# Laying the operand tiles of a split-float32 trunk at one residue modulo 512 bytes

## The chip, the cores and the metric

The kernel runs on one core of one Trainium2 chip. The metric is the device time of one execution in microseconds (us), lower is better; it is the median of several runs. A profile is one separate execution, recorded instruction by instruction.

## The reference, cut to what matters

One sequence of 512 tokens with 1024 channels goes through two layers, all in float32:

```python
# layer 0: RWKV-7 time mixing (six projections 1024x1024 or low rank, a recurrence per head of 64)
x = layer_norm(ALPHA * x + time_mix(x)) ; x = layer_norm(ALPHA * x + mlp(x, w1[0], w2[0]))
# layer 1: differential attention over shared K/V with a T5 bias, 16 score maps, 8 heads of 128
q = x @ w_q ; k, v = split(x @ w_kv)
attn = softmax(q1 k1 + bias) - lam * softmax(q2 k2 + bias)     # block-causal
x = layer_norm(ALPHA * x + (subln(attn @ v)) @ w_o) ; x = layer_norm(ALPHA * x + mlp(x, w1[1], w2[1]))
# mlp(x, w1, w2) = square(relu(x @ w1)) @ w2, w1 1024x4096, w2 4096x1024
```

## The kernel before

**Three products for one.** Every dense product is made of three TensorE matmuls on operands that were split into a high and a low part of type float32r (`split`, lines 105 to 107): high times high (line 141), high times low (line 142), low times high (line 143), all inside `mm3`. The first argument of a matmul is stationary (it is loaded into the array, 128 columns of 4 bytes, so 512 bytes in each partition), the second one is moving (512 or 256 columns). Three such matmuls are called a triple here.

**Where weights go.** `unit` loads 128x1024 weights into a `wst` tile (pool `ws`, 3 buffers), ScalarE rounds them into `whi` (line 106), and VectorE or GpSimd writes the rest into `wlo` (line 107). `whi` and `wlo` come from pool `wp` (4 buffers each) and, inside an MLP, four units in turn from pool `w4` (4 buffers each) and four from `wp`, beginning with `w4`. In the first MLP product and the attention projections the weights are stationary and `ba` (the transposed input, high and low) moves; in the second MLP product the activations `hh` and `hl` are stationary and the weights move; in attention's output product `yh` and `yl` are stationary and the weights move. Attention's scores use `qT` (stationary) and `kT` (moving).

**The first product after a norm** is computed in two halves of 256 tokens (`proj_halves`), so that it can begin before the last two token blocks are normalised: 288 matmuls of 256 columns in an MLP, 192 in attention.

**Where tiles lie.** SBUF pools are stacks: a pool opened later lies behind those still open, on memory of pools that are closed. A pool lays its tags one behind the other in the order of first use, each with its number of buffers, sizes rounded up to 32 bytes. `t` (line 83) asks for 128-byte alignment for the tags in `ALIGNED`; such a tag takes a further 128 bytes of its pool, so that `wlo`, `hl` and `yl` begin 128 bytes off where `whi`, `hh` and `yh` do. In the program as built, the tiles begin at these residues modulo 512: `ba` 384; `whi`/`wlo` in `w4` 256/384, in `wp` 384/0; `hh`/`hl` 0/128; `yh`/`yl` 256/384; `kT` and `qT` 128; in the first layer's projections the inputs `bb` 128, `bc` 160, `acc` 0 and the weights 256. Slices inside a tile are multiples of 512 bytes.

**What lies on what.** Attention's one pool `att` covers bytes 70656 to 174976: small set-up tiles (`rb`, `br`, `lm`, ...), `kT`, `qT`, `vt`, `bt`, and so on, with `yh` and `yl` last (150272 to 174976). The second MLP's pool `h` and its `w4` (140544 to 173440) lie on the same bytes, as the first MLP's do before attention. The order of the instructions on each engine is set by a scheduler that simulates the program; a tile in reused memory also waits for the last readers of what lay there.

**Order around the change.** The program is: first layer (`rwkv`), MLP 0 (`mlp(0, 1)`), attention, MLP 1. Attention projects groups of two heads (`P0` to `P3`), computes pairs (`p0` to `p3`), adds the output product of heads 0 to 3 in between (`o01`, `o23`), and ends with that of heads 4 to 7, one token block after the other, with the layer norm of each block behind it.

Of the kernel before, what the change touches and what calls it, by code (L numbers as in the profile page):

```python
# [9 lines left out]
F32R = mybir.dt.float32r  # L10
# [8 lines left out]
P = 128  # L19
D = 1024  # L20
T = 512
NT = T // P
# [3 lines left out]
HD = 64  # L26
NPAIR = 8
WCOL = 256
LINE = 128
ALIGNED = ("ba", "acc", "bb", "whi", "wlo", "hh", "hl", "yh", "yl")  # L30
ALPHA = 4.0 ** 0.25
CDEC = math.exp(-0.5)
GN_EPS = 64e-5
# [33 lines left out]
class Trunk:  # L67
# [15 lines left out]
    def t(self, pool, tag, shape, dt=F32, bufs=None):  # L83
        self.n += 1
        kw = {} if bufs is None else {"bufs": bufs}
        if tag in ALIGNED:
            kw["align_bytes"] = LINE
        return pool.tile(list(shape), dt, tag=tag, name=f"{tag}_{self.n}", **kw)

    def mul(self, eng, out, in0, in1):  # L90
# [59 lines left out]
    def setup(self):  # L150
        nc, a = self.nc, self.a
        cp = self.pool("const")
        self.cp = cp
        self.cst = self.t(cp, "cst", [P, NCST])
        self.cv = self.t(cp, "cv", [P, NVEC, NK])
        nc.sync.dma_start(out=self.cv, in_=a["cvec"])
        self.ident = self.cst[:, C_ID:C_ID + P]
        self.dr = self.pool("dr", space=DRAM)

    def wunit(self, src, kh, lo_eng=None):  # L160
# [10 lines left out]
    def rwkv(self):  # L171
# [12 lines left out]
        with ExitStack() as ph:  # L184
# [4 lines left out]
            ip = self.pool("inv", 1, ctx=ph)  # L189
# [178 lines left out]
            acc, wst, wos = [], {}, {}  # L368
# [52 lines left out]
            for step in PLAN.split():  # L421
# [21 lines left out]
                with ExitStack() as pri:  # L443
                    if off is not None:
# [3 lines left out]
                     "f": lambda g, b: self.finish(cm2, ep, psE, g, grp[g], b),  # L448
                     "l": load, "c": conv, "w": wo, "n": norm}[op](*z)
        self.lnp = self.pool("ln", 1, side="right")  # L450
        self.ws = self.pool("ws", 3, side="right")
        self.wp = self.pool("wp", 4, side="right")
        self.psT, self.tT = self.pool("psT", 2, space=PSUM), "t"
# [46 lines left out]
    def inverse(self, ip, GU, nbD, gbD, E):  # L500
        nc = self.nc
        V, S, G, PE = nc.vector, nc.scalar, nc.gpsimd, nc.tensor
        NU = self.t(ip, "nu", [P, 32, 32], bufs=2)
        nb = nbD.rearrange("u b s t -> (u b) (s t)")
        nc.sync.dma_start(out=NU.rearrange("p s t -> p (s t)"),
                          in_=bass.AP(tensor=nb.tensor, offset=nb.offset, ap=[[0, 2], [1024, 64], [1, 1024]]))
        for s in range(31):
            n, m = 31 - s, s // 2 + 1
            tm = self.t(ip, "gtm", [P, 144], bufs=3)
            tmv = tm[:, 0:m * n].rearrange("p (i t) -> p i t", t=n)  # L510
            gv = GU[:, 0:m, s + 1:32]
            E.tensor_tensor(out=tmv, in0=GU[:, 0:m, s:s + 1].to_broadcast([P, m, n]),  # L512
                            in1=NU[:, s:s + 1, s + 1:32].to_broadcast([P, m, n]), op=ALU.mult)
            E.tensor_tensor(out=gv, in0=gv, in1=tmv, op=ALU.add)  # L514
        for r in range(2):
            nc.sync.dma_start(out=gbD.rearrange("u b (j r) t -> r (u b) j t", r=2)[r], in_=GU[64 * r:64 * r + 64])
# [329 lines left out]
    def attention(self):  # L846
        nc, a = self.nc, self.a
        V, S, G, PE = nc.vector, nc.scalar, nc.gpsimd, nc.tensor
        with ExitStack() as ph:
            ap = self.pool("att", 1, ctx=ph)  # L850

            def ps_a():
                return self.t(self.psA, "a", [P, T])
# [31 lines left out]
            def project(g):  # L885
                wk = self.weight(a["kv"][g], G)
                wq = self.weight(a["q"][g], G)
                pss = self.proj_halves([wk, wq]) if g == 0 else None
                for i in range(4):
                    if g:  # L890
                        ps = ps_a()
                        self.proj_T((wk, wq)[i // 2], i % 2 * P, ps)
                    else:
                        ps = pss[i]
                    h = 2 * g + i % 2
                    if i < 2:
                        kt[h] = []
                        for s in range(2):
                            k = self.t(ap, "kT", [P, 2, T], F32R, bufs=7)
                            S.copy(out=k[R[s], 0], in_=ps[R[s]])  # L900
                            V.tensor_tensor(out=k[R[s], 1], in0=ps[R[s]], in1=k[R[s], 0], op=ALU.subtract)
                            nc.sync.dma_start(out=k[R[1 - s]].bitcast(F32), in_=k[R[s]].bitcast(F32))
                            kt[h].append(k)
                    else:
                        q = self.t(ap, "qT", [P, 2, T], F32R, bufs=4)
                        for s in range(2):
                            S.activation(out=q[R[s], s], in_=ps[R[s]], func=AF.Copy, scale=-SCALE)
                            V.scalar_tensor_tensor(out=q[R[1 - s], s], in0=ps[R[s]], scalar=-SCALE, in1=q[R[s], s],  # L908
                                                   op0=ALU.mult, op1=ALU.subtract)
                        qt[h] = q  # L910
                w = self.weight(a["kv"][4 + g], G)
                vt = self.t(ap, "vt", [P, NT, WCOL], bufs=2)
                for tt in range(NT):
                    ps = ps_a()
                    for k in range(NK):
                        self.mm3(ps[:, 0:WCOL], tuple(z[:, tt * P:(tt + 1) * P] for z in self.xk(k)), w[k],
                                 k == 0, k == NK - 1)
                    S.copy(out=vt[:, tt, :], in_=ps[:, 0:WCOL])
                vts[g] = vt
# [42 lines left out]
            def pair(g):  # L962
                bts = [bias(2 * g + f) for f in range(2)]
                pos = [self.t(self.psX, "o", [P, NT, P]) for _ in range(2)]
                ss = self.t(ap, "ss", [P, 2, NT], bufs=2)
                z = self.t(ap, "z", [P, 2, 2, NT], bufs=2)
                orow = [self.t(ap, "or", [P, NT, P], bufs=2) for _ in range(2)]
                for i in range(0, NT, NTAIL):
                    qbs = QB[i:i + NTAIL]
                    for qb in qbs:  # L970
                        for f in range(2):
                            block(2 * g + f, bts[f], pos[f], z, qb)
                        for f in range(2):
                            jk = self.t(ap, "jk", [P, P], bufs=2)
                            S.activation(out=jk, in_=pos[f][:, qb, :], func=AF.Square, accum_out=ss[:, f, qb:qb + 1])
                    sl = slice(min(qbs), max(qbs) + 1)
                    v = self.t(ap, "zi", [P, 2, NT], bufs=2)[:, :, sl]
                    V.scalar_tensor_tensor(out=v, in0=z[:, 0, :, sl], scalar=SUBLN_EPS, in1=z[:, 0, :, sl], op0=ALU.mult, op1=ALU.mult)
                    V.scalar_tensor_tensor(out=v, in0=ss[:, :, sl], scalar=1.0 / P, in1=v, op0=ALU.mult, op1=ALU.add)
                    rs = self.rsqrt(ap, "ar", v, [P, 2, len(qbs)])  # L980
                    for f in range(2):
                        for qb in sorted(qbs):
                            S.activation(out=orow[f][:, qb, :], in_=pos[f][:, qb, :], func=AF.Copy, scale=rs[:, f, qb - sl.start:qb - sl.start + 1])
                for f in range(2):
                    pt = self.t(self.psT, "t", [P, NT, P])
                    for qb in range(NT):
                        PE.transpose(pt[:, qb, :], orow[f][:, qb, :], self.ident)
                    hi = self.t(ap, "yh", [P, NT, P], F32R, bufs=6)
                    lo = self.t(ap, "yl", [P, NT, P], F32R, bufs=6)
                    S.activation(out=hi, in_=pt, func=AF.Copy, scale=sg)  # L990
                    V.scalar_tensor_tensor(out=lo, in0=pt, scalar=sg, in1=hi, op0=ALU.mult, op1=ALU.subtract)
                    ys[2 * g + f] = (hi, lo)
# [19 lines left out]
            for step in ATT.split():  # L1012
                hs = tuple(map(int, step[1:]))
                if step[0] == "o":
                    out_all(hs, 1.0 if done else ALPHA)
                    done.update(hs)
                else:
                    {"P": project, "p": pair}[step[0]](*hs)
# [92 lines left out]
```

## Time and profile before

| | us |
|---|---|
| median of 3 runs | 1554.7 (1552.41 to 1555.03) |
| profiled execution, its own time | 1556.39 |
| its span, first to last instruction | 1554.6 |
| TensorE matmul busy | 1418.8 (91%) |
| VectorE / ScalarE / GpSimd busy | 836.6 / 559.8 / 430.2 |

Matmuls are pipelined, so the length shown for one overlaps the next; a rate is read from one start to the next. The granted clock (PEclk) is a share of 2.4 GHz; half of it is 1.2 GHz.

### The profile page before, as it was taken

How to read it: one execution, taken by the hardware profiler on the slowest of the kernel's cores; microseconds unless marked ns; L12 is line 12 of the kernel's file. 1: busy time of each engine (PE TensorE's matmuls, PEld its weight loads, DVE VectorE, ACT ScalarE, POOL GpSimd, SP SyncE). 2: the span in 40 equal slices, each digit the busy share in tenths (PEclk: the TensorE clock that was granted, in tenths of full speed). 3: DMA queues.
4: the chain of work that ended last, by engine and by line, in shares of the span. 5: the costliest groups of instructions: out<-in, count | busy, mean ns of one | idle time of the engine just before them, and what ended most of it. 6: DMA issues, size and time to landing. Idle time of an engine off the chain costs nothing.

```text
span 1554.6 us, 21838 instructions
## 1 busy us (share of the span) xinstructions
PE 1418.8 (91%) x8296; PEld 1149.0 (74%) x8296; DVE 836.6 (54%) x1668; ACT 559.8 (36%) x1074; POOL 430.2 (28%) x383
## 2 busy tenths in 40 slices
PE   7879898966899699999999989999987999999997
PEld 2547587755766598888888887888876988888886
DVE  8965475665967853333333543456667433333346
ACT  2333343242333452322324244566445414232220
POOL 5764233273334430100101153322215201010010
PEclk9989889766889899999999999999988999999999
DMA  5245462324221343232323044323102433333311
GB/s 164 75 123 153 114 149 86 103 74 129 64 80 42 108 150 101 89 102 88 102 88 104 6 129 129 84 66 109 62 28 85 161 96 93 97 94 96 94 41 54
DMA packets 89121, 148.15 MB, mean 95 GB/s; under 512 B 34313, under 2 KB 48041, under 8 KB 89017
## 3 DMA queue, kind: packets, MB, share of 16 engines
q1 hardware_dynamic: 89016, 146.76, 31.9%
q8 instruction: 65, 1.06, 0.3%
q14 instruction: 40, 0.32, 0.1%
HBM read 127.74 MB, written 10.57 MB: 89 GB/s over the span
## 4 chain that ended last, share of the span: by engine, by line
PE 71%; DVE 15%; DMA 7%; ACT 2%; POOL 2%; issue 2%; SPq 1%; DVEq 0%; POOLq 0%; ACTq 0%
PE a L141 10%; PE a L142 10%; PE a L143 10%; PE o L142 5%; PE o L143 5%; PE o L141 5%; PE s L142 5%; PE s L143 5%; PE s L141 5%; DMA nu<-nbD 3%; PE e L474 1%; DVE ba L265 1%; PE o L960 1%; DVE gtm L512 1%; DVE gu L514 1%
## 5 line engine op out<-in xcount | busy, mean ns | idle before, releaser
L106 ACT CAST whi<-wst 128x1024 fp32r<-128x1024 f32 (+1 forms) x208 | 195.0, 949 | 356.9 <-PE a L143 139.5
L107 DVE TENSOR_TENSOR wlo<-wst,whi 128x1024 fp32r<-128x1024 f32 x120 | 151.1, 1259 | 231.5 <-ACT whi L106 231.5
L107 POOL TENSOR_TENSOR wlo<-wst,whi 128x512 fp32r<-128x512 f32 (+1 forms) x88 | 166.7, 1909 | 245.0 <-ACT whi L106 236.8
L91 POOL TENSOR_TENSOR r<-r 128x512 f32<-128x512 f32 x64 | 69.0, 1079 | 534.9 <-ACT hh L820 532.4
L822 DVE TENSOR_TENSOR hl<-r,hh 128x512 fp32r<-128x512 f32 x64 | 45.8, 717 | 147.3 <-POOL r L91 147.3
L141 PE MATMUL a<-ba,whi 128*128 128x512 f32 (+1 forms) x336 | 122.5, 366 | 2.2 <-DVE qT L908 2.2
L143 PE MATMUL a<-ba,wlo 128*128 128x512 f32 (+1 forms) x336 | 123.7, 369 | 0.0
L142 PE MATMUL a<-ba,whi 128*128 128x512 f32 (+1 forms) x336 | 123.2, 367 | 0.0
L143 PE MATMUL s<-ba,wlo 128*128 128x512 f32 (+1 forms) x232 | 82.2, 355 | 0.0
L142 PE MATMUL s<-ba,whi 128*128 128x512 f32 (+1 forms) x232 | 81.9, 353 | 0.2 <-DVE ba L107 0.2
L141 PE MATMUL a<-whi,ba 128*128 128x256 f32 x256 | 76.4, 298 | 5.8 <-ACT ev L315 3.2
L141 PE MATMUL s<-ba,whi 128*128 128x512 f32 (+1 forms) x232 | 80.9, 350 | 0.0
L142 PE MATMUL a<-wlo,ba 128*128 128x256 f32 x256 | 75.5, 295 | 0.0
L141 PEld LDWEIGHTS a<-ba,whi 128*128 128x128 f32 x336 | 64.7, 193 | 13.7 <-issue 2.2
L143 PE MATMUL a<-whi,ba 128*128 128x256 f32 x256 | 74.7, 292 | 0.0
L141 PE MATMUL o<-ba,whi 128*128 128x512 f32 (+1 forms) x200 | 71.8, 359 | 2.2 <-ACT ba L106 2.2
L143 PE MATMUL o<-ba,wlo 128*128 128x512 f32 (+1 forms) x200 | 72.6, 363 | 0.0
L142 PE MATMUL o<-ba,whi 128*128 128x512 f32 (+1 forms) x200 | 72.5, 363 | 0.0
L142 PEld LDWEIGHTS a<-ba,whi 128*128 128x128 f32 x336 | 64.2, 191 | 10.3
L143 PEld LDWEIGHTS a<-ba,wlo 128*128 128x128 f32 x336 | 64.2, 191 | 9.9
L141 PE MATMUL o<-whi,hh 128*128 128x512 f32 x176 | 69.3, 394 | 0.0
L142 PE MATMUL o<-wlo,hh 128*128 128x512 f32 x176 | 69.1, 393 | 0.0
(376 smaller groups left out, 3545.9 us busy)
## 6 DMA issues: line engine op xcount, KB each, us to landing
wst<-in_m SPq DMA_DIRECT2D x128, 512.0 KB, 3.9
wst<-in_kv SPq DMA_DIRECT2D x16, 512.0 KB, 4.3
wst<-in_wk SPq DMA_DIRECT2D x16, 256.0 KB, 3.4
wst<-in_wr SPq DMA_DIRECT2D x16, 256.0 KB, 3.5
wst<-in_wv SPq DMA_DIRECT2D x16, 256.0 KB, 4.0
wst<-in_q SPq DMA_DIRECT2D x8, 512.0 KB, 4.7
kT<-kT SPq DMA_DIRECT2D x16, 256.0 KB, 4.6
wst<-in_wo SPq DMA_DIRECT2D x8, 512.0 KB, 3.3
```

The lines of the kernel that those rows point to most:

```text
L91: return eng.tensor_tensor(out=out, in0=in0, in1=in1, op=ALU.mult)
L106: self.nc.scalar.copy(out=hi, in_=src)
L107: (lo_eng or self.nc.vector).tensor_tensor(out=lo, in0=src, in1=hi, op=ALU.subtract)
L141: mm(ps, lh, rh, start=first, stop=False)
L142: mm(ps, lh, rl, start=False, stop=False)
L143: mm(ps, ll, rh, start=False, stop=last)
L265: V.scalar_tensor_tensor(out=mx, in0=xx, scalar=cv[:, V_MU + i, c:c + 1], in1=x0, op0=ALU.mult, op1=ALU.add)
L474: PE.matmul(ps[:, c, :], d["bk"][hs, 4 * b + c].rearrange("p a t -> p (a t)"), d["ar"][hs, 4 * b + c].rearrange("p a t -> p (a t)"), start ...
L512: E.tensor_tensor(out=tmv, in0=GU[:, 0:m, s:s + 1].to_broadcast([P, m, n]), in1=NU[:, s:s + 1, s + 1:32].to_broadcast([P, m, n]), op=ALU.mult)
L514: E.tensor_tensor(out=gv, in0=gv, in1=tmv, op=ALU.add)
L822: V.tensor_tensor(out=hl, in0=r, in1=hh, op=ALU.subtract)
L960: PE.matmul(po[:, qb, :], at[:, kb, :], vt[:, kb, f * P:(f + 1) * P], start=(kb == 0), stop=(kb == qb))
```

## The change

Alignment by request goes away. Instead, three pads shift whole pools: 46 floats at the end of the pool `const`, 8 floats at the start of the pool `ln`, and a scratch tile of the first layer that is 32 bytes smaller (three buffers). Attention's matmul operands `kT`, `qT`, `yh` and `yl` move to a pool of their own, `attq`, opened before `att`. No instruction of any engine is added or removed apart from this.

```diff
-LINE = 128
-ALIGNED = ("ba", "acc", "bb", "whi", "wlo", "hh", "hl", "yh", "yl")
@@ t
-        if tag in ALIGNED:
-            kw["align_bytes"] = LINE
@@ setup
         self.ident = self.cst[:, C_ID:C_ID + P]
+        self.t(cp, "pad", [P, 46])
@@ rwkv
         self.lnp = self.pool("ln", 1, side="right")
+        self.t(self.lnp, "pad", [P, 8])
@@ inverse
-            tm = self.t(ip, "gtm", [P, 144], bufs=3)
+            tm = self.t(ip, "gtm", [P, 136], bufs=3)
@@ attention
+            aq = self.pool("attq", 1, ctx=ph)
             ap = self.pool("att", 1, ctx=ph)
...
-                            k = self.t(ap, "kT", [P, 2, T], F32R, bufs=7)
+                            k = self.t(aq, "kT", [P, 2, T], F32R, bufs=7)
...
-                        q = self.t(ap, "qT", [P, 2, T], F32R, bufs=4)
+                        q = self.t(aq, "qT", [P, 2, T], F32R, bufs=4)
...
-                    hi = self.t(ap, "yh", [P, NT, P], F32R, bufs=6)
-                    lo = self.t(ap, "yl", [P, NT, P], F32R, bufs=6)
+                    hi = self.t(aq, "yh", [P, NT, P], F32R, bufs=6)
+                    lo = self.t(aq, "yl", [P, NT, P], F32R, bufs=6)
```

## Rows read from the trace of the kernel before

**Rows 1.** the page's parts 1 and 4: busy time, and the chain that ended last
```profile
PE 1418.8 (91%) x8296; PEld 1149.0 (74%) x8296; DVE 836.6 (54%) x1668; ACT 559.8 (36%) x1074; POOL 430.2 (28%) x383
...
PE 71%; DVE 15%; DMA 7%; ACT 2%; POOL 2%; issue 2%; SPq 1%; DVEq 0%; POOLq 0%; ACTq 0%
```
**Rows 2.** windows by stage: us, busy and count per engine, PEclk, DMA share, GB/s
```profile
0.00:550.00 550.00, 455.20 (x3492) 341.73 (x3492) 386.73 (x835) 195.59 (x411) 249.86 (x266) 0.85 0.38 106
...
578.00:889.00 311.00, 311.00 (x1355) 253.14 (x1354) 115.98 (x154) 90.23 (x116) 31.64 (x31) 1.00 0.28 87
...
1149.00:1205.00 56.00, 44.12 (x251) 38.98 (x252) 42.66 (x90) 21.97 (x37) 21.81 (x12) 0.84 0.18 60
1205.00:1518.00 313.00, 313.00 (x1430) 258.01 (x1430) 113.01 (x131) 96.55 (x120) 33.84 (x32) 1.00 0.31 96
```
**Rows 3.** windows of four runs of 96 matmuls each, columns as above
```profile
583.99:606.18 22.19, 22.19 (x98) 18.03 (x96) 7.47 (x8) 5.29 (x6) 1.04 (x1) 1.00 0.37 116
606.18:628.20 22.02, 22.02 (x98) 18.01 (x97) 7.64 (x9) 4.20 (x4) 0.00 (x0) 1.00 0.31 94
628.20:650.59 22.39, 22.39 (x97) 18.03 (x96) 7.87 (x9) 7.82 (x11) 3.12 (x3) 1.00 0.25 75
650.59:672.78 22.19, 22.19 (x97) 18.15 (x96) 7.67 (x8) 8.93 (x13) 4.16 (x4) 1.00 0.32 95
```
**Rows 4.** timeline, TensorE, 628 to 673: start, length, line, tiles, shape
```profile
628.20 0.39 PE L141 MATMUL s<-ba,whi 128*128 128x512 f32 x1
...
650.59 0.39 PE L141 MATMUL o<-ba,whi 128*128 128x512 f32 x1
...
672.09 0.39 PE L141 MATMUL o<-ba,whi 128*128 128x512 f32 x1
672.31 0.40 PE L142 MATMUL o<-ba,whi 128*128 128x512 f32 x1
672.54 0.40 PE L143 MATMUL o<-ba,wlo 128*128 128x512 f32 x1
```
**Rows 5.** timeline, TensorE, first layer's key projection, columns as above
```profile
69.23 0.39 PE L142 MATMUL a<-bb,whi 128*128 128x512 f32 x1
...
78.76 0.40 PE L142 MATMUL a<-bb,whi 128*128 128x512 f32 x1
```
**Rows 6.** timeline, TensorE, 256-column matmuls of the second MLP's start
```profile
1203.53 0.28 PE L141 MATMUL a<-ba,whi 128*128 128x256 f32 x1
...
1206.26 0.28 PE L143 MATMUL a<-ba,wlo 128*128 128x256 f32 x1
```
**Rows 7.** window from the last output matmul to the second MLP's full-width ones
```profile
1171.90:1223.22 51.32, 39.98 (x313) 39.33 (x312) 32.20 (x48) 28.45 (x44) 24.82 (x15) 0.87 0.43 140
```
**Rows 8.** TensorE's waits, 1149 to 1205: total, times, longest
```profile
PE t L779 <- DVE ba L107: 9.0, 1, 9.0
```
**Rows 9.** timeline, ScalarE, around the end of attention
```profile
1148.02 1.41 ACT L990 ACTIVATE yh<-t,sg 128x512 fp32r<-128x512 f32 x2
...
1171.99 2.92 ACT L106 CAST whi<-wst 128x1024 fp32r<-128x1024 f32 x3
```
**Rows 10.** timeline, GpSimd, around the end of attention
```profile
1166.72 1.29 POOL L91 TENSOR_TENSOR acc<-acc,gb 128x512 f32<-128x512 f32 x1 [28.76 <-PE t L779]
...
1174.59 4.65 POOL L107 TENSOR_TENSOR wlo<-wst,whi 128x1024 fp32r<-128x1024 f32 x2
```
**Rows 11.** timeline, VectorE, around the end of attention
```profile
1148.79 1.43 DVE L991 SCALAR_TENSOR_TENSOR yl<-t,sg,yh 128x512 fp32r<-128x512 f32 x2 [2.82 <-ACT yh L990]
...
1177.00 2.25 DVE L102 SCALAR_TENSOR_TENSOR lr<-lr,lr 128x1 f32<-128x1 f32 x1
...
1183.39 0.16 DVE L100 TENSOR_TENSOR lr<-lr 128x1 f32<-128x1 f32 x1
```
**Rows 12.** timeline, the DMA queue's issues at the start of attention
```profile
896.90 0.42 SPq L856 DMA_DIRECT2D rb<-in_relb  x1
```
**Rows 13.** TensorE's waits, 889 to 925: total, times, longest
```profile
PE a L862 <- DMA br<-in_onehot: 2.5, 2, 2.2
```

## The prediction

> **What bounds the kernel now.** I read the page's busy times and its chain first [rows 1]: TensorE is busy for 91% of the span and holds 71% of the chain. The table by stage [rows 2] then shows where that is literally so: in the two MLPs, 578 to 889 and 1205 to 1518, TensorE is never idle, its granted clock is 1.00, and VectorE, ScalarE and GpSimd are each busy for under 40% of the time. There the time is the number of matmuls times the step from one start to the next. In the first layer (0 to 550) it is busy for 83% and waits for others; at the norms between stages, as 1149 to 1205, for 79%, at a clock of 0.84.
>
> So the question is what the step is, and whether it hangs on where operands lie. At 2.4 GHz 512 columns would need 213 ns. Four neighbouring runs of 96 matmuls [rows 3], with the same shapes, clock and count, last 22.19, 22.02, 22.39 and 22.19 us, so the mean step is 231.1, 229.4, 233.2 and 231.1 ns. They are, in this order, the second product with weights in `w4` (C) and in `wp` (D), and the first product with weights in `w4` (A) and in `wp` (B). Every later run of a kind repeats its time within 0.05 us. A and B run the same code on the same input; they differ in the pool of the weights, that is in the residue.
>
> The single steps [rows 4] (the first and last rows of A's and B's 96 each) tell more. In B, line 141 to line 142 keeps both stationary tiles and both moving tiles at residue 384: 226.7 ns on average over the run's 32 triples. Line 142 to 143, where the stationary residue goes from 384 to 0, takes 232.3, and 143 back to 141 takes 234.5. In A the same three steps, with weights at 256, 256 and 384 against an input at 384, take 232.0, 233.0 and 234.9. Constant but unequal residues stand by themselves in the first layer's key projection (input 128, weights 256): 41 steps from 69.23 to 78.76 are 232.4 ns each [rows 5]. So: constant and equal 227, constant and unequal 232, changing 227 to 235.
>
> **The change part by part.**
>
> *Residues.* Adding up the pools of the changed code: `const` ends at 21504, which is 42 times 512, so `ba` and `acc` are at 0; `h` begins at 70656 with `hh` and `hl` at 0; `w4` begins at 140288, `wp` at 175616, and `kT`, `qT`, `yh`, `yl` begin at 70656 in the new pool: all at 0. Without the extra 128 bytes per tag, high and low parts agree. Every full-width step of MLPs and attention's dense products then is of the kind "constant and equal". I take 227.2 ns for it (all B runs together; single runs lie between 226.7 and 228.5). The matmuls of 512 columns: A 2 layers x 288 = 576; B 2 x 336 in the MLPs and 288 in attention = 960; C and D 768 each; attention's output 192, taken at D's rate. Saved: 576 x 6.0 = 3.5 us, 960 x 3.9 = 3.7, 768 x 3.9 = 3.0, 768 x 2.2 = 1.7, 192 x 2.2 = 0.4; together 12.3 us, all but some 1.5 of it in the stages that TensorE bounds [rows 2]. The bounds: all 3264 steps at the shortest step that comes often (224 ns, line 141 to 142 in C's run of [rows 3]) would save 22.7 against today's mean of 231.0; all at A's dearest step (234.9) would cost 12.7. I take 12.3, since B's step is the one row that has what the change makes of all.
>
> The Trainium skill speaks against this: by *TensorE: Matmul & The Clock Gate*, Step-by-step, the array has two independent SBUF read ports, and loading the next tile's weights takes no read bandwidth from the running matmul. By that rule addresses would not matter and the term would be 0; the 1.0 us between A and D [rows 3] disagrees, though these rows do not exclude another cause than a shared port.
>
> *Half-width matmuls.* The 256-column ones step at 118.7 ns [rows 6] (24 of them, 2.73 us for 23 steps), and within 2 ns of that in B-like and A-like places alike: I give them 0, and 2 ns x 768 = 1.5 us either way.
>
> *First layer.* Its tiles do not go to 0: `bb`, `bc` and the weights of `wp1` come to 480, `acc` to 0. The key projection becomes equal (192 steps, 232 to 227, 1.0 us), the receptance projection stays mixed; both lie where TensorE waits for others a sixth of the time, so 0, with 1 us either way. The smaller `gtm` still holds its largest product (8 x 17); VectorE's instructions on it are the same.
>
> *What lies on what: attention to MLP 1.* Today MLP 1's `w4` lies on `yh` and `yl`, which are read until the last output matmul ends at 1171.9. The first three roundings into `whi` come at 1171.99, directly behind [rows 9], though ScalarE ran little after the two `yh` at 1148; GpSimd had stood still for 28.8 us before its first norm product, and its `wlo` work begins at 1174.59 [rows 10]. It then runs beside the last norms, and VectorE's 128x1 steps on two SBUF inputs last up to 2.25 us where they take 0.16 otherwise [rows 11]; TensorE waits 9.0 us for that chain [rows 8]. From 1171.90 to 1223.22, 51.3 us [rows 7], it has 288 half-width matmuls (34.2 at 118.7 ns) and some 3 us of transposes to do: 14 us are lost. In the changed layout `w4` (140288 to 173056) lies on `vt`, `bt`, `or`, `sc` and the set-up tiles alone; the last to be touched is `sg`, read by `yl` until 1150.2 [rows 11]. So rounding and `wlo` can go 22 us earlier, onto idle engines. What is late next is VectorE's chain of norms: GpSimd's four `wlo` of some 2.3 us will collide with it earlier instead, and hold back the eviction that frees PSUM. The gain lies between 0 (the scheduler leaves the order) and 11 (the 14 less the half tile's real wait for its norm); I take 5.
>
> *MLP 0 to attention.* The set-up DMAs (`rb` first, at 896.90 [rows 12]) now lie on `w4`, whose last readers end with the first half of the last token block some 5 us before, instead of on `r` and `hh`. Queued behind them on the same queue are the next weight loads. TensorE's 2.5 us of waiting for the one-hot tiles [rows 13] could go, or double if they come later in the queue: -2.5 to +5, and I take a gain of 1.
>
> Sum: 12.3 + 5 + 1 = 18.3 us off the profiled execution's 1556.4, so 1538.1. The median of the runs shown lies 1.7 below that execution: 1536.4, forecast as 1536.
>
> **The rivals.**
>
> *The residue is not the cause.* By the ports rule, or if the steps follow something else that differs between the pools, the term of 12.3 goes and what lies on what is left: 1554.7 less 0 to 6, so 1549 to 1555. For it: B's other two steps and C and D don't order by any simple rule of equality (D, with unequal neighbours, is the fastest mean). Against it: the two constant cases, 227 and 232, with nothing between.
>
> *Equal residues collide.* If a matmul's reads and the load of the next stationary tile meet in the same place, every step becomes like the dearest one, 234.9 ns. That costs 12.7 us, less the 6 of the other terms: 1561, slower than before. It decides as soon as the mean step is above 231.0 + 6.0/3264 = 232.8 ns. For it: in A and B the step from 143 to 141, the dearest, is one in which the running matmul and the next stationary tile lie at different residues in A but at the same in B (384 and 384, 234.5). Against it: B's 226.7.
>
> *The set-up tiles come late.* They wait for `w4`, fall behind weight loads, and TensorE, which has their matmuls among its dense ones, waits 5 us more; the other junction gains nothing: 1554.7 - 12.3 + 5 = 1547.
>
> **How the numbers follow.** The forecast (12.3 us from the step, between 0 and 11 at the junctions) has 0.70; its own range is 1526 to 1545. The ports rule or another cause has 0.13, the collision 0.09, the late set-up 0.08. A difference under 0.2%, 3.1 us, can't be told from none here. Faster: 0.68 of the forecast, 0.05 of the first rival, 0.05 of the third, 0.78. Same: 0.02, 0.06, 0.02 and 0.01, 0.11. Slower: 0.02 of the first, 0.07 of the second, 0.02 of the third, 0.11. The range for eight in ten is 1524 to 1553: below, the step at 224 ns or both junctions won in full; above, the first rival with little from the junctions.
>
> **What would show it.** In the MLPs of the changed kernel all four kinds of run should take the same time, 96 x 227.2 = 21.8 us; if A and B still differ by 0.2 us, or runs take 22.3 and more, the step is wrong. The three steps of a triple should be equal within 2 ns. At the second junction ScalarE should round into `whi` before 1165 (less what was won until then), TensorE's wait of 9.0 should shrink below 4, and VectorE's two-microsecond steps should come earlier. At the first, `rb` should be issued before the last output matmul of MLP 0. The prediction is wrong if the MLP stages keep their 311 and 313 us, and wrong in its second part if the roundings stay behind the last output matmul.

## The result, and the profile after

The changed kernel takes 1536.84 us (median of 4 runs, 1533.28 to 1539.69) against 1554.87 (1552.41 to 1555.76): a ratio of 0.9885, 95% interval 0.9861 to 0.9910. The forecast was 1536. The profiled execution took 1537.76 us, its span is 1535.8, that is 18.7 us less than before.

The page first: busy time and the chain, to be read beside [rows 1].

```profile
PE 1410.0 (92%) x8296; PEld 1151.9 (75%) x8296; DVE 829.9 (54%) x1668; ACT 561.0 (37%) x1074; POOL 430.6 (28%) x383
...
PE 72%; DVE 14%; DMA 7%; POOL 3%; ACT 2%; issue 2%; SPq 0%; DVEq 0%; ACTq 0%; POOLq 0%
```

The kernel still is bound by TensorE and executes the same instructions; TensorE is busy 8.8 us less, VectorE 6.7 us less. The windows by stage (columns as in [rows 2]) say where:

```profile
0.00:550.00 550.00, 459.07 (x3485) 345.73 (x3486) 385.77 (x834) 195.55 (x412) 250.22 (x265) 0.84 0.38 106
578.00:889.00 311.00, 311.00 (x1381) 257.68 (x1380) 121.42 (x170) 92.77 (x119) 33.28 (x32) 1.00 0.28 88
1149.00:1205.00 56.00, 49.00 (x330) 44.88 (x329) 36.13 (x87) 25.71 (x42) 17.22 (x13) 0.91 0.31 97
1205.00:1518.00 313.00, 313.00 (x1406) 260.24 (x1405) 120.60 (x155) 90.00 (x111) 30.57 (x29) 1.00 0.29 90
```

The same 311 us of the first MLP at the same clock hold 1381 matmuls where they held 1355: the step is shorter. In 1149 to 1205, the windows cut at other work now, so landmarks are better. From the first to the last matmul of each kind, in the two traces:

| stretch, us | before | after | |
|---|---|---|---|
| start to first full-width matmul of MLP 0 | 572.88 | 573.65 | +0.77 |
| from there to its last matmul | 324.22 | 318.11 | -6.11 |
| to the first score of attention | 37.94 | 38.02 | +0.08 |
| first to last score | 204.62 | 200.84 | -3.78 |
| to the last output matmul of attention | 32.03 | 32.85 | +0.82 |
| to the first full-width matmul of MLP 1 | 51.55 | 47.27 | -4.28 |
| from there to the last matmul | 321.58 | 315.32 | -6.26 |
| tail | 9.80 | 9.79 | -0.01 |

So 12.4 of the 18.7 us come from the MLPs' step, 4.3 from the junction before MLP 1, and 3.8 from the head of attention's scores. Four neighbouring runs of 96 matmuls, C, D, A and B as in [rows 3]:

```profile
584.56:606.32 21.76, 21.76 (x98) 18.02 (x97) 7.44 (x8) 5.32 (x6) 1.04 (x1) 1.00 0.37 117
606.32:628.08 21.76, 21.76 (x98) 18.02 (x97) 7.63 (x9) 4.22 (x4) 0.00 (x0) 1.00 0.31 96
628.08:649.84 21.76, 21.76 (x98) 18.02 (x97) 7.86 (x9) 7.84 (x11) 3.13 (x3) 1.00 0.26 78
649.84:671.60 21.76, 21.76 (x98) 18.02 (x97) 7.67 (x8) 8.93 (x13) 4.17 (x4) 1.00 0.32 97
```

All four take 21.76 us, 226.67 ns a step, and so does every other run of 96 of these kinds. Inside a run the three steps are equal too. The first and the last triple of B's run, and the matmul that follows it (timeline of TensorE, as [rows 4]):

```profile
649.84 0.39 PE L137 MATMUL o<-ba,whi 128*128 128x512 f32 x1
650.06 0.39 PE L138 MATMUL o<-ba,whi 128*128 128x512 f32 x1
650.29 0.39 PE L139 MATMUL o<-ba,wlo 128*128 128x512 f32 x1
...
670.92 0.39 PE L137 MATMUL o<-ba,whi 128*128 128x512 f32 x1
671.14 0.39 PE L138 MATMUL o<-ba,whi 128*128 128x512 f32 x1
671.37 0.39 PE L139 MATMUL o<-ba,wlo 128*128 128x512 f32 x1
671.60 0.39 PE L137 MATMUL s<-whi,hh 128*128 128x512 f32 x1
```

Over all runs of B the three steps have the means 226.7, 226.5 and 226.8 ns. Before, they were 226.7, 232.5 and 234.4.

### The profile page after: what moved, and what is told of

The parts are those of the page before. It is cut to its first block, busy times and chain, and to the rows that moved or that the text cites. A ratio compares the mean times of both kernels' runs of the same rounds, so it can differ in the third digit from the quotient of the medians.

```text
span 1535.8 us, 21834 instructions
## 1 busy us (share of the span) xinstructions
PE 1410.0 (92%) x8296; PEld 1151.9 (75%) x8296; DVE 829.9 (54%) x1668; ACT 561.0 (37%) x1074; POOL 430.6 (28%) x383
## 4 chain that ended last, share of the span: by engine, by line
PE 72%; DVE 14%; DMA 7%; POOL 3%; ACT 2%; issue 2%; SPq 0%; DVEq 0%; ACTq 0%; POOLq 0%
PE a L137 11%; PE a L138 10%; PE a L139 10%; PE o L138 5%; PE o L139 5%; PE o L137 5%; PE s L138 5%; PE s L139 5%; PE s L137 5%; DMA nu<-nbD 3%; PE e L472 2%; DVE ba L262 1%; DMA gbD<-gu 1%; PE o L959 1%; DVE gtm L510 1%
```

## The experiments

A word on distance: it is the start of a matmul's weights in SBUF less the start of its other operand, modulo 512 bytes. Each kernel was timed beside the kernel before on its chip (medians 1551 to 1553 us there). A step's mean is taken from the starts of the matmuls in the unbroken runs of its kind in both MLPs, that is without the last group of the second product, in which C and D take turns every 24 matmuls; A and B have stationary weights, C and D moving ones; A and C take them from `w4`, B and D from `wp`.

**1. The residues alone.** The changed kernel with attention's operands back in one pool, so that MLP 1's `w4` lies on `yh` and `yl` again, at equal residues.

```diff
-            aq = self.pool("attq", 1, ctx=ph)
-            ap = self.pool("att", 1, ctx=ph)
+            ap = aq = self.pool("att", 1, ctx=ph)
+            self.t(ap, "pad", [P, 96])
...
+                    if not ys:
+                        self.t(ap, "pad2", [P, 96])
```

> The changed kernel with attention's operand tiles put back into the one pool att, behind its other tiles, with two pads so that they stay at residue 0; the second MLP's w4 lies on yh and yl again, as before the change. Theory 1 (the step goes to 227 ns because stationary and moving tiles begin at one residue, and the junction before the second MLP is a second, separate gain that comes from what w4 lies on): all runs of 96 matmuls last 21.8 us, the stretch from the last output matmul to the first full-width matmul of the second MLP is back near 51.5 us (47.3 in the changed kernel), and the time is 1537 + 4 = 1541 us. Theory 2 (the order and the overlay make the whole gain): 1555 us. Theory 3 (the residue makes the whole gain, the junction follows it by chance): 1537 us.

Measured: 1539.52 us, ratio 0.9914 (0.9891 to 0.9938). Every step 226.67 ns, the MLP stretches 318.11 and 315.32, as in the changed kernel to the hundredth. The junction before MLP 1 is 51.91 us and the scores take 204.32, both as before the change.

**2. The pool alone.** The kernel before with `attq`, nothing else.

```diff
+            aq = self.pool("attq", 1, ctx=ph)
...
-                            k = self.t(ap, "kT", [P, 2, T], F32R, bufs=7)
+                            k = self.t(aq, "kT", [P, 2, T], F32R, bufs=7)
```

(and the same for `qT`, `yh` and `yl`)

> The kernel before with nothing changed but the new pool for kT, qT, yh and yl; the 128-byte alignment and the residues of ba, whi, wlo, hh and hl stay. Theory 1: runs of 96 matmuls keep their four times (22.19, 22.02, 22.39, 22.19 us), the roundings into whi come some 20 us before the last output matmul, the stretch before the second MLP's full-width matmuls goes from 51.5 to about 47.3 us, and the time is 1555 - 4 = 1551 us. Theory 2: 1537 us. Theory 3: 1555 us, stretch 51.5 us.

Measured: 1545.97 us, ratio 0.9950 (0.9933 to 0.9968). The steps are those of before, 231.2, 229.3, 233.3 and 231.2 for C, D, A, B, and so are the MLP stretches (324.22 and 321.58). The junction falls to 46.05 us, the scores to 201.17. The two parts of the change are cleanly apart: the step belongs to the residues, the junction and, which I had not expected, the head of the scores to the pool. By the medians the two parts add up to 1.36% where the whole change gives 1.15%, which the intervals allow.

**3. All at 32.** Every operand of the dense matmuls at residue 32.

```diff
-        self.t(cp, "pad", [P, 46])
+        self.t(cp, "pad", [P, 54])
...
-        self.t(self.lnp, "pad", [P, 8])
```

> The changed kernel with every pool that holds dense operands of MLPs and attention moved by 32 bytes, so that all of them begin at residue 32 in place of 0 (the first layer's bb, bc and weights come to 0). If only equality counts: steps 226.7 ns, runs 21.76 us, 1537 us. If tiles have to begin on a multiple of 512 (or of 64) bytes: steps of 230 and more, runs of 22.1 us and more, MLP stages of 317 and 320 us again, 1549 us or more.

Measured: 1535.43 us, ratio 0.9884 (0.9864 to 0.9903), all steps 226.67 ns, the MLP stretches 318.09 and 315.32. Being a multiple of 512 is worth nothing; being equal is.

**4. `w4` at distance 32, `wp` at 64.** Constant residues, no change within a triple.

```diff
+        self.t(self.w4, "pad", [P, 8], bufs=1)
...
-        self.t(self.lnp, "pad", [P, 8])
+        self.t(self.lnp, "pad", [P, 120])
```

> The changed kernel with the weights in w4 moved to residue 32 and those in wp to 64, all else at 0: four kinds of run, each at a constant difference, high and low parts equal. If any difference costs: steps of about 232 ns in all four kinds (runs of 22.3 us), the MLPs 16 us longer, 1553 us. If only differences of 128 and more cost: 226.7 ns and 1537 us. If it depends on which operand is behind: the kinds with weights stationary and with weights moving differ.

Measured: 1547.25 us, ratio 0.9972 (0.9955 to 0.9990); MLP stretches 325.48 and 322.79. Windows of four runs of 96, C, D, A, B:

```profile
578.51:600.90 22.39, 22.39 (x98) 18.00 (x97) 7.47 (x8) 5.28 (x6) 1.04 (x1) 1.00 0.35 117
600.90:622.87 21.97, 21.97 (x98) 18.03 (x96) 7.63 (x9) 4.21 (x4) 0.00 (x0) 1.00 0.29 95
622.87:645.26 22.39, 22.39 (x97) 18.03 (x96) 7.87 (x9) 7.82 (x11) 3.12 (x3) 1.00 0.23 73
645.26:667.67 22.41, 22.41 (x98) 18.05 (x96) 7.67 (x8) 8.92 (x13) 4.16 (x4) 1.00 0.29 94
```

C, A and B take 233.2 to 233.4 ns a step, as much as A, the dearest kind before the change. A constant distance of 32 bytes costs 6.6 ns a step. D, distance 64 with the weights moving, is the odd one at 228.9. This kernel loses the residues' whole gain and 1.2 us more in each MLP, and keeps the pool's.

**5. `w4` at distance 128, `wp` at 256.**

```diff
+        self.t(self.w4, "pad", [P, 32], bufs=1)
...
-        self.t(self.lnp, "pad", [P, 8])
+        self.t(self.lnp, "pad", [P, 72])
```

> The changed kernel with the MLPs' weights moved away from the inputs by more than a stationary tile's small step: those in w4 lie at residue 128, those in wp at 256, inputs and activations at 0. Theory 'equal modulo 512': only the same residue gives the short step, so all four kinds of run are long again as with 32 and 64: weights stationary 232 to 234 ns per step, weights moving 228 to 234; each full-width MLP stretch 322 to 326 us instead of 318.1 and 315.3; the whole 1545 to 1549 us. Rival 'equal modulo 128' (or 64): all four kinds keep 226.7 ns and the whole stays at 1537 us. A third possibility, that the price grows with the distance: 256 dearer than 128, and both dearer than the 233.3 ns of distances 32 and 64.

Measured: 1543.11 us, ratio 0.9941 (0.9918 to 0.9964). The windows of C, D, A, B:

```profile
582.32:604.72 22.40, 22.40 (x98) 18.02 (x97) 7.48 (x8) 5.30 (x6) 1.04 (x1) 1.00 0.34 117
604.72:626.50 21.78, 21.78 (x98) 18.02 (x97) 7.62 (x9) 4.21 (x4) 0.00 (x0) 1.00 0.29 96
626.50:648.81 22.31, 22.31 (x97) 18.08 (x96) 7.86 (x9) 7.82 (x11) 3.13 (x3) 1.00 0.23 73
648.81:670.60 21.79, 21.79 (x97) 18.02 (x96) 7.67 (x8) 8.92 (x13) 4.17 (x4) 1.00 0.30 97
```

Neither theory had this: 128 is as dear as 32 (233.3 with the weights moving, 232.4 with the weights stationary), and 256 is as cheap as 0 (226.9 and 227.0). "Equal modulo 512" is wrong, and "equal modulo 128" as well.

**6. High and low 128 apart in `w4`, `wp` at distance 384.**

```diff
         hi = self.t(wp, "whi", [P, D], F32R)
+        if wp is self.w4 and self.nw == NW + 1:
+            self.t(wp, "pad", [P, 32], bufs=1)
...
-        self.t(self.lnp, "pad", [P, 8])
+        self.t(self.lnp, "pad", [P, 40])
```

> The changed kernel with a gap of 128 bytes between high and low weights in w4 (high 0, low 128, as the kernel before has one), and the weights in wp constant at 384; inputs and activations at 0. Theory 'equal modulo 512, step by step': in the first product with weights in w4 the step between two high weights (line 137 to 138) keeps 226.7 ns, the two steps that touch the low weights take 232 to 235, the mean is 230 to 232; with weights in wp all three steps take 232 to 234. With weights moving the means are 229 to 232. The whole is 1544 to 1548 us. Rival 'the change between high and low is what costs, not the distance between the two operands': wp, which is constant, keeps 226.7 ns, only w4 is dearer, and the whole is 1541 us.

Measured: 1546.07 us, ratio 0.9971 (0.9955 to 0.9988). A's three steps are 227.7, 232.4 and 234.1 ns, the pattern that B had before the change; the two steps that touch the matmul with the low weights are the dear ones, though no other matmul has its operands apart. `wp`, constant at 384, takes 232.3 (B) and 233.1 (D): the rival that only the jump costs has fallen. With the weights moving, C takes 229.0 ns in five of its six runs of 96 and 233.2 in the first one of MLP 0, at the same residues; so the price of a mixed triple isn't fixed by the residues alone, and what else sets it is not shown.

**9. Residues 0 and 256 in `w4`, `wp` at 288.** The theory formed from 5: equal modulo 256. Experiment 6 with a gap of 64 floats in place of 32, and a pad of 64 floats in `ln`.

```diff
+        if wp is self.w4 and self.nw == NW + 1:
+            self.t(wp, "pad", [P, 64], bufs=1)
...
-        self.t(self.lnp, "pad", [P, 8])
+        self.t(self.lnp, "pad", [P, 64])
```

> The changed kernel with the weights in w4 split over two residues that are 256 apart (high 0, low 256) and those in wp constant at 288, which is 256 + 32; inputs and activations at 0. Theory 'equal modulo 256', formed after the distances 128, 256 and 384: both kinds of run with weights in w4 keep 226.7 to 227 ns although the residue changes within each triple, and both kinds with weights in wp take what distance 32 took, 233 ns; MLP stretches 321.5 to 323 and 319 to 320.5 us, the whole 1541 to 1545 us. Rival 'a constant distance of 256 happens to be harmless, but a change of residue costs by itself': w4 also takes 229 to 235 ns, and the whole is 1545 to 1549 us.

Measured: 1542.29 us, ratio 0.9945 (0.9924 to 0.9966). C, D, A, B:

```profile
584.81:606.59 21.78, 21.78 (x97) 18.02 (x96) 7.43 (x8) 5.29 (x6) 1.04 (x1) 1.00 0.36 120
606.59:628.99 22.40, 22.40 (x97) 18.00 (x96) 7.66 (x9) 4.20 (x4) 0.00 (x0) 1.00 0.28 94
628.99:650.80 21.81, 21.81 (x98) 18.02 (x96) 7.85 (x9) 7.84 (x11) 3.12 (x3) 1.00 0.23 74
650.80:673.19 22.39, 22.39 (x97) 18.04 (x96) 7.67 (x8) 8.90 (x13) 4.16 (x4) 1.00 0.29 94
```

C and A take 226.7 and 227.1 ns although the low weights lie 256 bytes off the high ones, B and D take 233.3 and 233.4. The MLP stretches, 323.01 and 320.34, are in the expected range (the first at its edge). So a triple is short when the two operands of each of its matmuls begin at one residue modulo 256, and a change of residue by 256 inside the triple costs nothing. That each matmul has its price for itself is not shown: in A of experiment 6 the step in front of the one matmul apart is long as well.

**7 and 8. The first layer at 0 as well, and the changed kernel again.** For 7, three more pads bring `bb`, `bc`, `acc` and `wp1` to residue 0.

```diff
+            if not self.padded:
+                self.padded = 1
+                self.t(ip, "pad", [P, 56])
...
+        av = self.t(ep, "av", [P, T], bufs=2)
...
-        av = self.t(ep, "av", [P, T], bufs=2)
...
+        if not p:
+            self.t(ep, "pad", [P, 80])
```

> The changed kernel with the first layer's dense operands (bb, bc, the weights in wp1 and acc) brought to residue 0 too, by three more pads. Theory 'equal modulo 512': the receptance and the output projection, 192 steps each, fall from 230 to 235 ns to 226.7, so TensorE has some 2 us less to do there; as TensorE waits for other engines in that stage, the whole gains 0 to 2 us against the changed kernel (1535 to 1537). Rival 'the stage is bound by the other engines': those steps are shorter and the time of the first layer is the same within what it varies between executions; the whole is 1537 us.

> The changed kernel once more, to compare the others with on the same chip: 1537 us, a ratio of 0.9885 to the kernel before, 226.7 ns per full-width step of the MLPs. The first layer's length is what each theory leaves free: if it varies between executions of one kernel, it comes anywhere between 568 and 574 us.

Measured: 1533.08 us for 7 (ratio 0.9881, 0.9860 to 0.9903) and 1532.27 for 8 (0.9882, 0.9862 to 0.9902): the same. In the receptance projection the mean falls from 231.4 to 229.4 ns (some 145 steps between 215 and 245 ns in each trace) and not to the 226.7 expected; in the first layer's output projection, which was expected to shorten too, it stays (231.6 and 231.7 ns, some 125 steps). The first layer ends at 571.36 against 571.32. The rival holds in so far as shorter steps there shorten nothing; why the output projection keeps its steps at equal residues is not shown. Experiment 8 also gives what one execution differs from another: the MLP stretches are again 318.11 and 315.32, the first layer's end is 571.32 where it was 573.65.

**10. The head of the scores.** Experiments 1 and 2 gave the 3.5 us there to the pool. The traces show a pair of instructions that could be why. In experiment 1 (the residues alone; VectorE and then GpSimd, timeline), as in the kernel before, the add that masks the bias, both inputs in SBUF, starts beside a `wlo` of GpSimd and ends with it:

```profile
923.66 2.27 DVE L928 TENSOR_TENSOR bt<-bt,am 128x128 f32<-128x128 f32 x1 [2.54 <-ACT bt L927]
925.85 0.28 DVE L929 COPY bt<-bt 128x256 f32<-128x256 f32 x1
926.16 0.69 DVE L907 SCALAR_TENSOR_TENSOR qT<-a,qT 64x512 fp32r<-64x512 f32 x1
926.89 0.29 DVE L928 TENSOR_TENSOR bt<-bt,am 128x128 f32<-128x128 f32 x1
```
```profile
923.43 2.35 POOL L103 TENSOR_TENSOR wlo<-wst,whi 128x1024 fp32r<-128x1024 f32 x1 [1.87 <-ACT whi L102]
```

`qT` stands behind it, and TensorE waits 2.6 us for `qT`. In the changed kernel, with the second pool, the `wlo` comes earlier, the add takes 1.22, and TensorE's longest wait there is 0.8. To test it, experiment 1 with the add reading PSUM instead of one SBUF operand:

```diff
-                S.copy(out=bt[:, 256:T], in_=ps[:, 0:256])
-                V.tensor_tensor(out=bt[:, T - P:T], in0=bt[:, T - P:T], in1=am, op=ALU.add)
+                S.copy(out=bt[:, 256:T - P], in_=ps[:, 0:P])
+                V.tensor_tensor(out=bt[:, T - P:T], in0=ps[:, P:256], in1=am, op=ALU.add)
```

> The kernel with the residues alone (attention's operands in the single pool, as in the first experiment), with one edit in the bias of a head: the masked block is added from PSUM (ps + am) where it was added in SBUF (bt + am), so VectorE's instruction reads one SBUF operand less and doesn't wait for that part of ScalarE's copy. Theory 'the 3.5 us at the head of the scores are a collision of that instruction with GpSimd's wlo': it takes 0.3 to 0.7 us where it took 2.27, qT comes earlier, and the scores take 201 us (204.32 without the edit); the whole 1536 against 1539.5. Rival 'the order of GpSimd's and VectorE's other work holds the scores up': the instruction is short and the scores stay within 0.7 us of 204.3.

Measured: 1539.43 us, ratio 0.9925 (0.9902 to 0.9948), scores 203.51. The add is short now, and the copy behind it is held in its place (the `wlo` beside it runs from 926.14 for 2.36):

```profile
926.26 0.29 DVE L928 TENSOR_TENSOR bt<-s,am 128x128 f32<-128x128 f32 x1 [2.27 <-ACT bt L927]
926.47 2.18 DVE L929 COPY bt<-bt 128x256 f32<-128x256 f32 x1
928.68 0.69 DVE L907 SCALAR_TENSOR_TENSOR qT<-a,qT 64x512 fp32r<-64x512 f32 x1
```

By its numbers the expectation of the collision failed: I had looked at one instruction, and the next one was of the same kind. TensorE still waits 2.1 us for `qT`. Behind this wait its granted clock falls to 0.50 for 3.41 us, as it does in the kernel before and in experiment 1 (waits of 2.6 us); in the changed kernel and in experiments 2, 8 and 11, where no wait there is over 0.8 us, it stays at 1.00. Windows (columns as in [rows 2]) of the kernel before, experiments 1 and 10, and, at the same place, the changed kernel:

```profile
938.21:941.62 3.41, 3.26 (x15) 3.29 (x16) 1.20 (x5) 0.81 (x2) 0.00 (x0) 0.50 0.44 160
926.50:929.91 3.41, 2.91 (x13) 2.94 (x14) 1.55 (x5) 0.82 (x2) 0.00 (x0) 0.50 0.59 210
929.51:932.92 3.41, 3.41 (x16) 3.41 (x17) 0.99 (x4) 0.82 (x2) 0.00 (x0) 0.50 0.56 182
932.61:936.02 3.41, 3.41 (x30) 3.41 (x30) 0.99 (x4) 1.14 (x3) 0.00 (x0) 1.00 0.48 156
```

The 256-column matmuls in these windows step at 213 ns at 0.50 and at 120 ns at 1.00. As an estimate, 16 steps of 93 ns more make 1.5 us, so such a wait costs more than its own length, and shortening it from 2.6 to 2.1 us keeps that part.

**11. The same edit in the changed kernel.**

> The changed kernel with the same edit of the bias. Theory 'collision': the instruction falls from 1.22 us at the head of the scores to 0.3 to 0.7, for one head of eight; gain 0 to 1 us, 1532 to 1537 us, scores 200 to 201 us. Rival 'the order': nothing moves, or the scheduler's new order costs up to 3 us at the head of the scores.

Measured: 1533.23 us, ratio 0.9882 (0.9864 to 0.9900), scores 199.69 instead of 200.8 to 201.0. That is just over the 0 to 1 us expected, and too little for the median to show. There, too, the copy is held (1.02 us).

**12. Both instructions on PSUM,** in the single pool:

```diff
-                V.tensor_copy(out=bt[:, 0:256], in_=bt[:, 256:257].to_broadcast([P, 256]))
+                V.tensor_copy(out=bt[:, 0:256], in_=ps[:, 0:1].to_broadcast([P, 256]))
```

> The kernel of the run before last (residues alone, masked block added from PSUM) with the second bias instruction also reading PSUM: the copy that spreads the first column over 256 columns, which had taken over the 2.18 us from the add before it. Theory 'collision': whichever VectorE instruction with only SBUF operands stands beside GpSimd's wlo is held to its end; with both reading PSUM none is left, the two take 0.3 us each, qT is written some 1.9 us earlier, TensorE's wait of 2.1 us for it falls below 0.7, and the scores take 201 to 202 us (203.51 and 204.32 before). The whole is 1536 to 1538 us against 1539.4. Rival 'the held instruction is only what happens to stand there, and an instruction that writes SBUF is held as well': the copy still takes 1 to 2.2 us, and the scores stay at 203 to 204.5. Rival 'order': both are short and TensorE's wait goes to another engine; scores above 203.

Measured: 1537.24 us, ratio 0.9906 (0.9885 to 0.9927); scores 199.80. VectorE, GpSimd and TensorE's waits:

```profile
924.85 0.29 DVE L928 TENSOR_TENSOR bt<-s,am 128x128 f32<-128x128 f32 x1 [2.20 <-ACT bt L927]
925.05 0.41 DVE L929 COPY bt<-s 128x256 f32<-128x256 f32 x1
925.50 0.69 DVE L907 SCALAR_TENSOR_TENSOR qT<-a,qT 64x512 fp32r<-64x512 f32 x1
```
```profile
924.73 2.37 POOL L103 TENSOR_TENSOR wlo<-wst,whi 128x1024 fp32r<-128x1024 f32 x1 [1.64 <-PE s L926]
```
```profile
PE s L939 <- ACT qT L906: 0.8, 1, 0.8
```

The `wlo` stands at the same place beside the same two instructions, which now take 0.29 and 0.41 us. TensorE no longer waits for VectorE's `qT`, and its clock stays at 1.00 at the place where it fell before:

```profile
928.39:931.80 3.41, 3.41 (x31) 3.41 (x30) 0.00 (x0) 0.37 (x1) 0.00 (x0) 1.00 0.44 152
```

The scores fall by 4.5 us against experiment 1, to a little below what was expected, and by more than the pool gives. The wait of 2.6 us and the 1.5 estimated for the clock make 4.1 of them. That the head of the scores was held by this collision is shown. The medians of 12 and 1 (1537.24 and 1539.52) lie in overlapping intervals, so the profile shows the gain and the time alone would not. No kernel here beats the changed one: 7, 8 and 11 have one ratio within 0.0001. The changed kernel with both instructions on PSUM wasn't run.

## Why the prediction was right, point by point

**The step: right in place and size, with a wrong period.** Forecast 227.2 ns in all kinds, measured 226.67. The MLPs' 2784 full-width matmuls had a mean of 231.11 ns; 4.44 ns less is 12.4 us, and the two MLP stretches lost 6.11 and 6.26. The prediction had 10.8 of its 12.3 there, since it took B's 227.2, in which a few longer steps were left. The 1.5 it saw in attention are not to be seen: residues alone change the scores by 0.3 us and the stretch behind them by 0.1. The steps of attention's 512-column projections did fall, from 231.3 to 227.7 ns (some 250 adjacent steps in each trace); over 288 of them this is 1.0 us, and where the rest of it went, in a stage in which TensorE is busy for 95% of the time, is not shown. The steps of the output product stayed at 229.8 ns (some 145), although its operands now begin at one residue; why is not shown either.

The cases that the prediction could not order fall into place with the period of 256, which it took for 512. In D before the change, `hh` at 0 met `whi` at 384 (apart), `hh` 0 met `wlo` 0 and `hl` 128 met `whi` 384 (both equal modulo 256): two of three, 229.3 ns. B also had two (its low weights at 0 against 384 were 128 apart) and 231.2; C and A had one, 231.2 and 233.3; none gives 232.3 to 233.4 (experiments 4 to 6 and 9, but for D of experiment 4), three give 226.67. The price isn't a plain sum over the matmuls of a triple: with one apart, B had two of three steps longer, and A, with one equal, was no better than none; the step behind its equal matmul was its longest, 234.9 ns.

By the Trainium skill (*TensorE: Matmul & The Clock Gate*, Step-by-step) the stationary and the moving operand have two independent SBUF read ports. The rival that the prediction drew from this, that addresses would not matter, does not hold here: 226.67 against 233.3 ns for the same instructions at the same clock, by a shift of 32 bytes. What the two operands share, a port or something else, is not shown. The sign that the prediction gave against this rival was misread, though: between A and D of [rows 3] lie 0.37 us (22.39 and 22.02), not 1.0. The rival of the collision has fallen too: with equal residues no unbroken run's mean step in the MLPs is above 227.3.

**Half-width matmuls: 0 was nearly right.** The rows that answer to [rows 6], 23 steps apart (timeline of TensorE):

```profile
1189.74 0.28 PE L138 MATMUL s<-ba,whi 128*128 128x256 f32 x1
...
1192.50 0.28 PE L138 MATMUL a<-ba,whi 128*128 128x256 f32 x1
```

That is 120.0 ns against 118.7: equal residues cost 1.3 ns here, 1.0 us over 768 steps at most, inside the 1.5 either way. With 256 columns, then, equal residues are not the fastest: over some 700 such steps in each trace the mean is 119.9 ns with them, 118.8 before, and 116.3 in experiment 4 (distances 32 and 64).

**Attention to MLP 1: right, 4.3 us for 5.** `w4` no longer waits for the output product. ScalarE's three roundings and GpSimd's `wlo` (timeline; [rows 9] and [rows 10] had them at 1171.99 and 1174.59, behind the last output matmul at 1171.7) start 22 us ahead of that matmul, at 1163.5:

```profile
1141.12 2.94 ACT L102 CAST whi<-wst 128x1024 fp32r<-128x1024 f32 x3 [0.82 <-DVE yl L990]
...
1142.25 7.09 POOL L103 TENSOR_TENSOR wlo<-wst,whi 128x1024 fp32r<-128x1024 f32 x3 [13.33 <-ACT whi L102]
```

TensorE's waits between the last output matmul and the full-width ones, where [rows 8] had 9.0 us for `ba`:

```profile
PE o L138 <- DVE ba L103: 3.6, 1, 3.6
PE o L137 <- ACT ba L102: 1.3, 1, 1.3
```

The wait is below the 4 us named, and VectorE's long steps moved ahead with GpSimd's work, as was said (timeline of VectorE; [rows 11]):

```profile
1147.22 2.67 DVE L757 SCALAR_TENSOR_TENSOR acc<-acc,mv,gb 128x512 f32<-128x512 f32 x1
...
1150.47 1.70 DVE L96 TENSOR_TENSOR lr<-lr 128x1 f32<-128x1 f32 x1
```

Experiments 1 and 2 show that it is the pool: 51.9 us without it, 46.1 with it alone. The prediction had no term for the clock, and it has a part: in this stretch it is at 0.50 for 13.65 us before, for 10.24 after, and for 6.83 in experiments 2, 3 and 11. The kernels with the new pool take 46.1 to 46.5 us here with 6.83 and 46.6 to 47.4 with 10.24, so that about 1 us here goes with the clock.

**MLP 0 to attention: the mechanism came, the gain of 1 us did not.** `rb` is issued at 881.26, ten microseconds before the last output matmul at 891.76, as forecast. But TensorE waits as long as in [rows 13]. The DMA queue's issues, then TensorE's first matmul on these tiles, then its wait:

```profile
881.26 0.34 SPq L855 DMA_DIRECT2D rb<-in_relb  x1
881.65 0.41 SPq L859 DMA_DIRECT2D br<-in_onehot  x1
...
892.55 0.33 SPq L859 DMA_DIRECT2D br<-in_onehot  x1
```
```profile
892.08 0.43 PE L861 MATMUL a<-br,rb 32*8 32x160 f32 x2
```
```profile
PE a L861 <- DMA br<-in_onehot: 2.6, 1, 2.6
```

The second one-hot tile is issued only behind the first one's matmul, at 892.08; `br` has two buffers, and the result of that matmul takes the other. 2.6 us later, at 895.2, it lands. The prediction counted the first of four loads; the limit was the tag's number of buffers. This is read from the traces; more buffers weren't tried.

**Attention's scores: 3.8 us that no step of the prediction had.** They are the pool's (experiment 2: 3.5) by the collision of experiments 10 to 12: a wait of 2.6 us, and behind it 3.41 us at half the clock, both gone. The prediction had used the same collision at the next junction and not looked for it here. That the total came out this close is luck, as sums cancel: these 3.8 and 1.6 more from the MLPs, 5.4 us, stand against 1.5 that attention's residues did not give, 1.1 missed ahead of attention, 0.7 at the junction, 0.8 behind the scores and a first layer that ended 0.8 later, 4.9 us. The difference, 0.5, is that of the span: 18.7 us where 18.3 were forecast.

**First layer: 0, right.** It ended 0.77 us later in this pair of traces, and at 567.3 to 573.7 us over all the kernels here, wherever its tiles lay. The differences go, though not in strict order, with the time that TensorE spends at half the clock there: 146.8 us where it ended at 567.7 (experiment 2), 174.1 where it ended at 573.7 (experiment 11).

## What to carry to other kernels

Where TensorE is the bound, read the step from one start to the next per kind of run, not the busy share; if runs of one shape and clock differ by 1 or 2%, compare the start addresses of the stationary and the moving operand modulo 256 bytes and make them equal, by pads rather than by an alignment that shifts each tag. When tiles move to other pools, look at what they then lie on: who may start earlier, and which VectorE instructions with only SBUF operands that work will then meet on GpSimd. Where TensorE waits for a microsecond or two between dense stretches, look at the granted clock behind the wait before pricing it.

## What the runs showed of the hardware that was not expected

- Step of a 512-column float32r matmul with a new 128x128 stationary tile each time, at granted clock 1.00, by distance modulo 512: 0: 226.67 ns; 256: 226.7 to 227.1; 32: 233.2 to 233.3; 128: 232.4 to 233.3; 288: 233.3 to 233.4; 384: 232.3 to 233.1; 64: 233.4 with the weights stationary, but 228.9 with them moving. The price doesn't grow with the distance. What the two operands share is not shown, nor is the case of 64 explained. These are steps of the MLPs; the output products of attention (229.8 ns) and of the first layer (231.7 in experiment 7) stay longer at equal residues, and with 256 columns no gain is seen.
- A wait of TensorE of 2.1 to 2.6 us at the head of the scores was followed by 3.41 us at granted clock 0.50 in all three kernels that had it, and in none of the five compared with them whose waits there were 0.8 us or less.
- At equal residues 226.67 and 120.0 ns are 512 and 256 columns at 2.4 GHz plus 13.3 ns each, as worked out from these rows.
- A VectorE instruction whose operands all lie in SBUF, an add of two tiles or a copy, was held to the end of the GpSimd `wlo` beside it: 2.27 and 2.18 us where they take 0.28 to 0.29 alone. With an input from PSUM the two took 0.29 and 0.41 beside the same `wlo`. The Trainium skill (*SBUF — State Buffer*, Who interferes with whom) says this: two SBUF inputs, or a copy in a two-port mode, contend with a GpSimd instruction that reads SBUF, and whichever comes second is blocked throughout; these rows agree.
